# Seven block products in place of eight for the projections vb and g of a hybrid encoder layer

## The chip, the core and the metric

The kernel runs on one core of one Trainium2 chip. The metric is the device time of one execution in microseconds (us). The kernel before has a median of 2027.04 us over three runs, from 2026.38 to 2032.31. One further execution was profiled, and took 2027.01 us.

## What is computed

The input x has 2048 rows (positions) of 1024 channels, in float32. One layer is computed:

```
y = rmsnorm(h, pre_mix_g);  z = y @ w_in
zu, zv, zq, zk, zvb, zg, zlr = split(z)      # widths 512, 512, 256, 256, 512, 512, 16
a = gmlp_mixer(zu, zv, ...)                  # blocks of 128 positions: gelu, layernorm, gate
b = gla_mixer(zq, zk, zvb, zg, zlr, ...)     # a state carried over chunks of 64 positions, times silu(zg)
m = concat(a, b) @ w_out
h = h + rmsnorm(m, post_mix_g)
f = square(relu(rmsnorm(h, pre_ff_g) @ w_ff1)) @ w_ff2
h = h + rmsnorm(f, post_ff_g)
```

The change touches the part `zvb`, `zg` of `z = y @ w_in`: for each block of 512 positions a matrix of 512 x 1024 (y) times one of 1024 x 1024 (the columns of vb and of g).

## The kernel before

The 2048 positions are worked off in four blocks of 512 (loop at L620), each as four tiles of 128. A block runs through stages in this order: vb, q, k, g, then the output projection of the block ahead of it (`out_proj`, L577), then v and u. Block 0 begins with g and vb and has no output projection. After the four blocks come the last output projection and the two feed-forward products, whose seven-product scheme (table `WINO`, L41) was there already.

Each stage is a `product` (L254): eight steps over the inner dimension, and in each step four tiles of three matmuls (`mm3`, L148: a float32 operand is split into a high part of reduced precision and a low rest, and high x low, high x high and low x high are added up). A stage of 512 columns is thus 96 matmuls of 128x512. The weights of a step are read into a staging tile (`stage`, L196: a ring of five, shared with the reads of x), cast by ScalarE to the high part and subtracted by VectorE to the low part (`load_w`, L209), into rings of six tiles each. The weights of q and k are split in block 0 only and written out; later blocks read both parts back (`load_q`, L227).

Results leave PSUM (eight banks, in two rings of four called mm and mx) by `keep` (L601): ScalarE for vb (copy), g (Silu), v and u (Gelu), VectorE for q and k.

Between the steps stand small jobs. `Jobs` (L60) holds generators; `tick` (L91) runs one or two of their steps after each step of a stage, and `finish` (L466) runs them without ticks until a named result is there. `gla` (L324) is the linear attention of one tile, in seven steps. They go from one engine to the next: `gt` on TensorE, then xs, Abs, Exp, Ln, lah and lal (L336 to L345), then `cm` and `dc` on TensorE, then three Exp and qe, ke, then the transposes `qk`, then `sc` and `up`, then `o`, a norm and the transposes `pt`. `spatial` (L435, matmuls `mixd`) and `gate` (L456, transposes `pt` of zu) are the other mixer; `hpost` (L489) closes a tile; `sums` (L534) builds sums of the feed-forward input. `lookup` (L311) puts the loads of ScalarE's function tables where Gelu, Silu and Exp/Ln change.

TensorE's order is the order in which the code is written. The other engines' orders in this part are set by a scheduler when the program is built; each engine and SyncE's queue of transfers then works strictly in that order.

Of the kernel before, what the change touches and what calls it, by code (L numbers as in the profile page):

```python
# [102 lines left out]
def trunk(  # L103
# [24 lines left out]
    q_d = {(g, k): dram.tile([P, 2, n], F32, name=f"{g}_d{k}") for g, n in (("q", 272), ("k", 256)) for k in range(KT)}  # L128

    o_d = [[dram.tile([P, 2, 512], F32, name=f"o_d{hf}_{k}") for k in range(KT)] for hf in range(2)]  # L130
    b_d = [[dram.tile([P, 4, H], F32, name=f"b_d{p}_{k}") for k in range(4)] for p in range(NP)]
    t_d = [{key: dram.tile([P, 2, 2, 512], F32, name=f"t_d{c}_{key}") for key in RIGHT} for c in range(NC)]

# [120 lines left out]
    def product(name, ks, lhs, rhs, evac, steps=1, before=None, tag="mm", later=None):  # L254

        pss = None
        for k in ks:
            if before:
                before(k)
            wh, wl = rhs(k)  # L260
            lh = [lhs(k, t) for t in range(TPB)]
            if pss is None:
                pss = [bank(f"pp_{name}_{t}", tag) for t in range(TPB)]
            for t in range(TPB):
                mm3(pss[t][:, :wh.shape[-1]], *lh[t], wh, wl, k == ks[0], k == ks[-1])
            if k == ks[-1]:
                if later is not None:
                    later.extend((evac, t, pss[t][:, :wh.shape[-1]]) for t in range(TPB))
                else:
                    for t in range(TPB):  # L270
                        evac(t, pss[t][:, :wh.shape[-1]])
            jobs.tick(steps)

    def stats_x(b):

# [190 lines left out]
    def finish(b, part):  # L466

        while b >= 0 and any((i, part) not in ab for i in range(b * TPB, (b + 1) * TPB)):
            if not jobs.step():
                jobs.now += 1  # L470
# [57 lines left out]
    def plus(eng, out_, x_, y_):  # L528
        eng.tensor_tensor(out_, x_, y_, ALU.add)  # L529

    def minus(eng, out_, x_, y_):
        return eng.tensor_tensor(out_, x_, y_, ALU.subtract)
# [82 lines left out]
    def group(b, g, func, before=None, tag="mm", later=None):  # L615
        product(f"{b}_{g}", range(KT), y(b),
                lambda k: load_q(b, g, k) if g in "qk" else load_w(f"{b}_{g}", w_in, GROUPS[g], k),
                keep(b, g, func), 2, before, tag, later)

    for b in range(NB):  # L620
        tiles = range(b * TPB, (b + 1) * TPB)
        if b == 0:
            stats = stats_x(0)


            kept = []
            group(b, "g", AF.Silu, later=kept)

            def before_vb(k):
                if k < 4:  # L630
                    next(stats, None)
                    next(stats, None)
                if k == 4:
                    for _ in stats:
                        pass
                    for evac, t, pst in kept:
                        evac(t, pst)

            group(b, "vb", AF.Copy, before_vb, "mx")
        else:  # L640
            if b == NB - 1:
                jobs.add(*((lambda k=k: sums(0, k), 1) for k in range(4)))
            group(b, "vb", AF.Copy)
        if b == 0:
            with tc.issue_after(loads["0_vb"]):
                consts()
        group(b, "q", None)
        group(b, "k", None)
        if b > 0:
            group(b, "g", AF.Silu, lambda k: finish(b - 1, 1) if k == KT - 1 else None)  # L650
        jobs.add(*((lambda i=i: gla(i), 2) for i in tiles))
        if b > 0:
            out_proj(b - 1)
            jobs.add(*((lambda i=i - TPB: hpost(i), 3) for i in tiles))
# [590 lines left out]
```

## Time and profile before

| what | value |
|---|---|
| median of three runs | 2027.04 us |
| profiled execution | 2027.01 us |
| its span, first to last instruction | 2024.9 us |
| mean granted TensorE clock | 0.995 |
| TensorE busy (matmul) | 1991.8 us, 98% |
| VectorE, ScalarE, GpSimd busy | 1354.9, 928.5, 287.4 us |
| read and written in HBM | 331.45 and 138.54 MB |

PE is TensorE's matmuls, PEld its weight loads, DVE VectorE, ACT ScalarE, POOL GpSimd and SP SyncE, which issues most transfers. A busy time counts every instant at which an instruction of the engine is under way. Since matmuls overlap, the mean duration of one (some 390 ns for 128x512) is longer than the step from one to the next; the steps are read from stretches of time.

### The profile page before, as it was taken

The numbers are of one execution on the slowest core, as the hardware profiler recorded it, in microseconds if no ns is written. First come the engines' busy times: TensorE is split into PE (matmuls) and PEld (weight loads), VectorE is DVE, ScalarE is ACT, GpSimd is POOL, SyncE is SP. The second block draws the span as 40 slices with busy tenths as digits, with TensorE's granted clock in tenths as the row PEclk, the third lists the DMA queues.
The fourth block names the chain that finished last, engine by engine and source line by source line (L and its number), as shares of the span: only waits on it lengthen the run. The fifth ranks groups of instructions, "written<-read, shape, count | busy, mean of one in ns | idle before, by whom it ended". The sixth has DMA issues, their size and how long they took to land.

```text
span 2024.9 us, 27423 instructions
## 1 busy us (share of the span) xinstructions
PE 1991.8 (98%) x9504; PEld 1652.5 (82%) x9504; DVE 1354.9 (67%) x2369; ACT 928.5 (46%) x1846; POOL 287.4 (14%) x464
## 2 busy tenths in 40 slices
PE   8999999999999999999999999999999999999997
PEld 7989888988888887888887888888888887888886
DVE  4483467136724756657678777675888887888887
ACT  5462465136423546556668666665222214222212
POOL 1220312002100200003330333230000003000002
PEclk9999999999999999999999999999999999999999
DMA  7644745635883576758888887787676678867676
GB/s 241 203 131 154 233 157 168 200 135 157 263 281 110 164 278 216 266 171 289 279 280 297 297 291 285 267 278 272 229 257 249 237 275 251 268 246 266 238 266 180
DMA packets 178763, 471.83 MB, mean 233 GB/s; under 512 B 22320, under 2 KB 53568, under 8 KB 164928
## 3 DMA queue, kind: packets, MB, share of 16 engines
q1 hardware_dynamic: 147824, 373.45, 54.4%
q0 software_dynamic: 30800, 96.62, 14.4%
q8 instruction: 75, 1.23, 0.2%
q14 instruction: 64, 0.52, 0.1%
HBM read 331.45 MB, written 138.54 MB: 232 GB/s over the span
## 4 chain that ended last, share of the span: by engine, by line
PE 59%; DVE 1%; DMA 1%; ACT 1%; issue 0%; DVEq 0%; ACTq 0%
PE pf_A L149 6%; PE po_A L149 6%; PE pf_A L151 6%; PE po_A L150 6%; PE po_A L151 6%; PE pf_A L150 6%; PE po_C L149 3%; PE po_C L150 3%; PE po_C L151 3%; PE pf_C L149 3%; PE pf_C L151 3%; PE pf_C L150 3%; PE po_B L149 1%; PE po_B L150 1%; PE po_B L151 1%; PE pf_B L151 1%
## 5 line engine op out<-in xcount | busy, mean ns | idle before, releaser
L529 DVE TENSOR_TENSOR acc<-acc,po_A 128x512 f32<-128x512 f32 x232 | 159.7, 688 | 58.9 <-PE po_A L151 31.9
L980 ACT CAST sh_s<-r 128x512 fp32r<-128x512 f32 x96 | 55.5, 618 | 164.9 <-PE po_A L151 95.1
L980 ACT CAST sh_a<-f 128x512 fp32r<-128x512 f32 x94 | 54.6, 618 | 128.9 <-DMA f<-f_d 87.7
L146 DVE TENSOR_TENSOR wl_s<-s,wh_s 128x512 fp32r<-128x512 f32 x96 | 66.2, 689 | 61.9 <-ACT wh_s L743 61.8
L149 PE MATMUL pf_A<-hl_t,wh_s 128*128 128x512 f32 x256 | 102.0, 398 | 5.1 <-ACT uy L925 2.5
L149 PE MATMUL po_C<-tt,sh_s 128*128 128x512 f32 x256 | 101.2, 395 | 3.3 <-DMA tt<-t_d_t 3.3
L149 PE MATMUL pp_o<-wl_o,abh 128*128 128x512 f32 x256 | 102.9, 402 | 0.9 <-DVE h L486 0.8
L149 PE MATMUL po_A<-tt,sh_s 128*128 128x512 f32 x256 | 100.6, 393 | 1.0 <-DMA tt<-t_d_t 1.0
L151 PE MATMUL pf_A<-hh_t,wl_s 128*128 128x512 f32 x256 | 101.4, 396 | 0.0
L150 PE MATMUL po_C<-tt,sh_s 128*128 128x512 f32 x256 | 100.9, 394 | 0.0
L150 PE MATMUL pf_A<-hh_t,wh_s 128*128 128x512 f32 x256 | 100.7, 393 | 0.0
L151 PE MATMUL po_C<-tt,sl_s 128*128 128x512 f32 x256 | 100.5, 393 | 0.0
L150 PE MATMUL po_A<-tt,sh_s 128*128 128x512 f32 x256 | 100.2, 391 | 0.0
L151 PE MATMUL pp_o<-wh_o,abl 128*128 128x512 f32 x256 | 99.9, 390 | 0.0
L151 PE MATMUL po_A<-tt,sl_s 128*128 128x512 f32 x256 | 99.9, 390 | 0.0
L150 PE MATMUL pp_o<-wh_o,abh 128*128 128x512 f32 x256 | 99.7, 390 | 0.0
L529 DVE TENSOR_TENSOR acc<-acc,po_C 128x512 f32<-128x512 f32 x120 | 82.6, 688 | 23.6 <-PE po_C L151 15.9
L149 PE MATMUL po_A<-tt,sh_a 128*128 128x512 f32 x248 | 97.4, 393 | 0.0
L150 PE MATMUL po_A<-tt,sh_a 128*128 128x512 f32 x248 | 97.1, 391 | 0.0
L151 PE MATMUL po_A<-tt,sl_a 128*128 128x512 f32 x248 | 96.8, 390 | 0.0
L159 POOL TENSOR_TENSOR rs_f<-rs_f,mhalf 128x1 f32<-128x1 f32 x16 | 13.6, 847 | 574.1 <-DVE rs_f L158 574.0
L146 DVE TENSOR_TENSOR wl_a<-w1s,wh_a 128x512 fp32r<-128x512 f32 x96 | 65.9, 687 | 41.7 <-ACT wh_a L743 41.4
(303 smaller groups left out, 5909.2 us busy)
## 6 DMA issues: line engine op xcount, KB each, us to landing
tt<-t_d_t SPq DMA_DIRECT2D x61, 1024.0 KB, 5.2
tt<-t_d_b SPq DMA_DIRECT2D x46, 1024.0 KB, 4.8
w1s<-in_w SPq DMA_DIRECT2D x64, 512.0 KB, 4.9
f<-f_d SPq DMA_DIRECT2D x64, 512.0 KB, 7.1
w2s<-in_w POOLq DMA_DIRECT2D x32, 512.0 KB, 6.3
t_d_t<-th_t POOLq DMA_DIRECT2D x64, 256.0 KB, 5.0
t_d_t<-tl_t POOLq DMA_DIRECT2D x64, 256.0 KB, 4.7
f_d<-ux SPq DMA_DIRECT2D x30, 512.0 KB, 5.5
```

The lines of the kernel that those rows point to most:

```text
L146: v.tensor_tensor(out_lo, src, hi.bitcast(F32), ALU.subtract)
L149: pe.matmul(ps, ahi, blo, start=start, stop=False, **kw)
L150: pe.matmul(ps, ahi, bhi, start=False, stop=False, **kw)
L151: pe.matmul(ps, alo, bhi, start=False, stop=stop, **kw)
L159: pool.tensor_tensor(r, r, mhalf[:, :n], ALU.pow)
L529: eng.tensor_tensor(out_, x_, y_, ALU.add)
L980: a.copy(hi, src)
```

## The change

vb and g of blocks 1 to 3 are computed together, after q and k, as one product of 2x2 blocks with seven products of blocks (`pair`). A block product has four steps of two tiles of three matmuls, 24 in all. Its left operands are blocks of y and four sums of them (s1 to s4), made in q and k from fresh reads of x (`read_s`, `load_s`); its right operands are blocks of the weights and four sums (t1 to t4), which `sums_w` makes once as jobs of block 0 and writes to DRAM. Each of the 28 weight tiles of a pair is read, cast and split. Three PSUM chains, A, B and C, take the products up. Block 0 keeps its eight products. The jobs `sums(0, k)` of block 3 are added after the pair in place of ahead of vb. The new functions and the block loop:

```diff
+    PAIR = ("p1", "p2", "p5", "p6", "p7", "p4", "p3")
+    done_w = []
+    def sums_w(k):
+        bs_ = []
+        for c in range(2):
+            st = wp.tile([P, D], F32, name=f"vs{k}_{c}", tag="xr", bufs=4)
+            dma.dma_start(st, w_in[(k + 4 * c) * P:(k + 4 * c + 1) * P, 1536:2560])
+            bs_.append((st[:, 0:512], st[:, 512:D]))
+        (b11, b12), (b21, b22) = bs_
+        yield 5
+        t1, t2 = (wp.tile([P, 512], F32, name=f"vt{n}_{k}", tag="hts", bufs=2) for n in (1, 2))
+        minus(v, t1, b12, b11)
+        minus(v, t2, b22, t1)
+        minus(v, b12, b22, b12)
+        minus(v, b21, b21, t2)
+        for n, t in enumerate((t1, t2, b12, b21)):
+            dma.dma_start(v_d[k][:, n, :], t)
+        done_w.append(k)
+        yield 1
+    def read_s(b, k):
+        ts = stage(f"xs1_{b}_{k}"), stage(f"xs2_{b}_{k}")
+        for t, kk in zip(ts, (k, k + 4)):
+            dma.dma_start(t, xt[kk * P:(kk + 1) * P, b * TB:(b + 1) * TB])
+        return ts
+    def load_s(b, k, y1, y2):
+        for t, kk in ((y1, k), (y2, k + 4)):
+            a.activation(t, t, AF.Copy, scale=gpre[:, kk:kk + 1])
+        hi = wp.tile([P, D], F32R, name=f"sh{b}_{k}", tag="xr", bufs=4)
+        lo = wp.tile([P, D], F32R, name=f"sl{b}_{k}", tag="h", bufs=4)
+        (a11, a21), (a12, a22) = ((t[:, 0:256], t[:, 256:512]) for t in (y1, y2))
+        plus(v, a22, a21, a22)
+        minus(v, a21, a11, a21)
+        minus(v, a11, a22, a11)
+        minus(v, a12, a12, a11)
+        for n, t in enumerate((y1, y2)):
+            a.copy(hi[:, n * 512:(n + 1) * 512], t)
+            split_lo(lo[:, n * 512:(n + 1) * 512], t, hi[:, n * 512:(n + 1) * 512])
+        return hi, lo
+    def pair(b, ss_):
+        chains = {}
+        zv_, zg_ = {}, {}
+        i0 = b * TPB
+        for m, n in enumerate(PAIR):
+            left, right, chain = WINO[n]
+            begun = chain in chains
+            if not begun:
+                chains[chain] = [bank(f"pv{b}_{chain}{t}", "mx" if chain == "B" else "mm") for t in range(2)]
+            for k in range(4):
+                if right[0] == "t":
+                    st = stage(f"ws_{b}_{n}_{k}")
+                    loads[f"{b}_pair"] = dma.dma_start(st, v_d[k][:, int(right[1]) - 1, :]).ins
+                    wh = wq.tile([P, 512], F32R, name=f"wh_{b}_{n}_{k}", tag="wh", bufs=NW)
+                    wl = wq.tile([P, 512], F32R, name=f"wl_{b}_{n}_{k}", tag="wl", bufs=NW)
+                    a.copy(wh, st)
+                    split_lo(wl, st, wh)
+                else:
+                    wh, wl = load_w(f"{b}_{n}", w_in, GROUPS["vb" if right[2] == "1" else "g"],
+                                    k + 4 * (int(right[1]) - 1))
+                for t in range(2):
+                    if left[0] == "s":
+                        c0 = ("s2", "s3", "s4", "s1").index(left) * 256 + t * P
+                        lh = [z_[:, c0:c0 + P] for z_ in ss_[k]]
+                    else:
+                        c0 = (int(left[1]) - 1) * 256 + t * P
+                        lh = [z_[:, c0:c0 + P] for z_ in ys[b, k + 4 * (int(left[2]) - 1)]]
+                    mm3(chains[chain][t], *lh, wh, wl, k == 0 and not begun, k == 3, skip_group_check=True)
+                if k % 2:
+                    if n == "p6" and k == 3:
+                        finish(b - 1, 1)
+                    jobs.tick(2)
+            r = [rx[b][:, t:t + 1] for t in range(TPB)]
+            A, B, C = (chains.get(c) for c in "ABC")
+            for t in range(2):
+                if n == "p1":
+                    zv_[t] = slot(f"zvb_{i0 + t}")
+                    lookup(zv_[t], A[t], AF.Copy, scale=r[t])
+                elif n == "p2":
+                    v.scalar_tensor_tensor(zv_[t], B[t], r[t], zv_[t], ALU.mult, ALU.add)
+                elif n == "p6":
+                    zg_[t] = slot(f"zg_{i0 + t}", tag="four")
+                    a.copy(zg_[t], A[t])
+                elif n == "p7":
+                    zg_[t + 2] = slot(f"zg_{i0 + t + 2}", tag="four")
+                    a.copy(zg_[t + 2], A[t])
+                    plus(v, zg_[t + 2], zg_[t + 2], C[t])
+                elif n == "p4":
+                    zv_[t + 2] = slot(f"zvb_{i0 + t + 2}")
+                    lookup(zv_[t + 2], A[t], AF.Copy, scale=r[t + 2])
+                elif n == "p3":
+                    plus(v, zg_[t], zg_[t], C[t])
+        for t in range(TPB):
+            lookup(zg_[t], zg_[t], AF.Silu, scale=r[t])
+            z["vb", i0 + t], z["g", i0 + t] = zv_[t], zg_[t]
...
@@ -637,18 +744,32 @@
                         evac(t, pst)
 
             group(b, "vb", AF.Copy, before_vb, "mx")
-        else:
-            if b == NB - 1:
-                jobs.add(*((lambda k=k: sums(0, k), 1) for k in range(4)))
-            group(b, "vb", AF.Copy)
-        if b == 0:
             with tc.issue_after(loads["0_vb"]):
                 consts()
-        group(b, "q", None)
-        group(b, "k", None)
+        ss_, raw = [], []
+        def before_q(k):
+            if b > 0 and k in (2, 5):
+                raw.append(read_s(b, len(raw)))
+        def before_k(k):
+            if b > 0 and k % 2 == 0:
+                ss_.append(load_s(b, k // 2, *raw[k // 2]))
+                if len(raw) < 4:
+                    raw.append(read_s(b, len(raw)))
+        group(b, "q", None, before_q)
+        group(b, "k", None, before_k)
         if b > 0:
-            group(b, "g", AF.Silu, lambda k: finish(b - 1, 1) if k == KT - 1 else None)
+            while len(done_w) < 4:
+                if not jobs.step():
+                    jobs.now += 1
+            pair(b, ss_)
+        if b == NB - 1:
+            jobs.add(*((lambda k=k: sums(0, k), 1) for k in range(4)))
         jobs.add(*((lambda i=i: gla(i), 2) for i in tiles))
+        if b == 0:
+            jobs.add(*((lambda k=k: sums_w(k), 1) for k in range(4)))
         if b > 0:
             out_proj(b - 1)
             jobs.add(*((lambda i=i - TPB: hpost(i), 3) for i in tiles))
```

The end of block 0. TensorE's rows from the last matmul of u on, before: gt is the gate matmul of a gla tile, cm and dc its next step; the numbers behind the names are tile and buffer.

```order
L151 MATMUL pp_0_u_3_1287<-wh_0_u_7_1609,yl_0_7_411 128x512
L334 MATMUL gt2_1633<-gw_218,lrt2_1549 128x256
L334 MATMUL gt3_1647<-gw_218,lrt3_1553 128x256
L149 MATMUL pp_1_vb_0_1672<-wl_1_vb_0_1669,yh_1_0_1323 128x512
L150 MATMUL pp_1_vb_0_1672<-wh_1_vb_0_1668,yh_1_0_1323 128x512
...
L151 MATMUL pp_1_vb_3_1675<-wh_1_vb_2_1722,yl_1_2_1436 128x512
L350 MATMUL cm2_1738<-lal2_1644,trir_224 128x256
```

And now:

```order
L153 MATMUL pp_0_u_3_1295<-wh_0_u_7_1615,yl_0_7_415 128x512
L441 MATMUL gt3_1639<-gw_222,lrt3_1551 128x256
L457 MATMUL cm2_1678<-lal2_1597,trir_228 128x256
...
L463 MATMUL dc2_1683<-trir_228,lah2_1596 128x2
L556 MATMUL mixd2_1702<-zv_2_1251,wt_224 128x128 x4
L457 MATMUL cm3_1717<-lal3_1650,trir_228 128x256
...
L481 MATMUL qk2_1745<-ident_217,qe2_1696 128x128
...
L556 MATMUL mixd3_1754<-zv_3_1253,wt_224 128x128 x4
L151 MATMUL pp_1_q_0_1764<-wl_q1_0_1761,yh_1_0_1332 128x272
```

Between gt3 and cm2, and between cm2 and cm3, stood 36 matmuls of vb and none; now there is nothing between gt3 and cm2, and four small matmuls between cm2's step and cm3's. gt2 has moved one step of u up.

ScalarE at the same place, before (zu is the Gelu of u, e the Abs, Exp and Ln of a gla tile):

```order
L318 ACTIVATE zu_0_1625<-pp_0_u_0_1284,rx0_510 128x512
...
L318 ACTIVATE zu_3_1631<-pp_0_u_3_1287,rx0_510 128x512
L205 ACTIVATE yh_1_7_1662<-xt_1_7_1660,gpre_211 128x512
L338 ACTIVATE e2_1637<-xs2_1635 128x256
L317 ACT_TABLE_LOAD
L318 ACTIVATE e2_1637<-e2_1637 128x256
```

And now:

```order
L310 ACTIVATE xs1_1_1_1963<-xs1_1_1_1963,gpre_215 128x512
L445 ACTIVATE e2_1590<-xs2_1588 128x256
L424 ACT_TABLE_LOAD
L425 ACTIVATE e2_1590<-e2_1590 128x256
L425 ACT_TABLE_LOAD
L425 ACTIVATE zu_0_1631<-pp_0_u_0_1292,rx0_514 128x512
L425 ACT_TABLE_LOAD
L425 ACTIVATE e2_1590<-e2_1590 128x256
L425 ACT_TABLE_LOAD
L425 ACTIVATE zu_1_1633<-pp_0_u_1_1293,rx0_514 128x512
...
L445 ACTIVATE e3_1643<-xs3_1641 128x256
L424 ACT_TABLE_LOAD
```

One table load has become five; Exp and Ln of tile 2 now enclose the first Gelu of u. In the whole program the table loads go from 14 to 18.

VectorE at the end of q in block 2, before: zq takes q out of PSUM, abl is the low part of the transposes pt.

```order
L146 TENSOR_TENSOR abl6_0_3925<-pt6_0_3919,abh6_0_3924 128x512
L146 TENSOR_TENSOR abl7_0_3934<-pt7_0_3928,abh7_0_3933 128x512
L609 TENSOR_SCALAR zq_8_4149<-pp_2_q_0_4021,rx2_3744 128x272
L609 TENSOR_SCALAR zq_9_4151<-pp_2_q_1_4022,rx2_3744 128x272
```

And now (xs1, xs2 are the four blocks of x that become sums, sl their low parts):

```order
L148 TENSOR_TENSOR abl7_0_4111<-pt7_0_4105,abh7_0_4110 128x512
L639 TENSOR_TENSOR xs1_2_2_4202<-xs2_2_2_4203,xs1_2_2_4202 128x256
L639 TENSOR_TENSOR xs2_2_2_4203<-xs2_2_2_4203,xs1_2_2_4202 128x256
L148 TENSOR_TENSOR sl2_2_4293<-xs1_2_2_4202,sh2_2_4292 128x512
L148 TENSOR_TENSOR sl2_2_4293<-xs2_2_2_4203,sh2_2_4292 128x512
L636 TENSOR_TENSOR xs2_2_3_4255<-xs1_2_3_4254,xs2_2_3_4255 128x256
L639 TENSOR_TENSOR xs1_2_3_4254<-xs1_2_3_4254 128x256
L716 TENSOR_SCALAR zq_8_4182<-pp_2_q_0_3982,rx2_3925 128x272
```

The sums of y stand ahead of zq. The transposes pt4 and pt5 stood behind 36 matmuls of vb and now stand behind 36 of q.

## Rows read from the trace of the kernel before

**Rows 1.** Span and granted clock of the core:

```profile
core 0: 2024.9 us, clock 0.995
```

**Rows 2.** What TensorE waited for (total us, times, longest):

```profile
PE pp_g L149 <- ACT yh L205: 6.5, 1, 6.5
PE pp_vb L149 <- ACT zu L318: 0.3, 2, 0.2
```

**Rows 3.** Stretches (us): length, busy by engine (instructions), granted clock, DMA share, GB/s:

```profile
6.50:11.50 5.00, 4.95 (x12) 3.79 (x13) 4.15 (x6) 3.19 (x5) 0.00 (x0) 1.00 0.74 226
136.10:168.70 32.60, 32.60 (x186) 27.20 (x185) 17.05 (x43) 17.35 (x48) 4.21 (x6) 1.00 0.34 94
168.70:194.80 26.10, 25.64 (x212) 25.40 (x211) 10.31 (x25) 6.87 (x18) 2.02 (x2) 1.00 0.56 181
338.30:362.50 24.20, 24.18 (x114) 19.86 (x115) 10.89 (x23) 10.59 (x22) 3.11 (x4) 1.00 0.43 124
362.50:386.00 23.50, 23.50 (x193) 23.50 (x193) 5.52 (x11) 3.80 (x7) 0.00 (x0) 1.00 0.70 216
386.00:407.80 21.80, 21.80 (x98) 18.03 (x97) 3.22 (x6) 5.15 (x7) 0.00 (x0) 1.00 0.63 216
552.60:576.60 24.00, 23.77 (x194) 23.56 (x193) 10.13 (x19) 3.87 (x7) 0.00 (x0) 1.00 0.95 309
```

**Rows 4.** ScalarE in order of time, end of block 0: start, us, instruction:

```profile
134.90 1.84 ACT L318 ACTIVATE zu<-pp_u,rx 128x512 f32<-128x512 f32 x3
138.15 0.71 ACT L205 ACTIVATE yh<-xt,gpre 128x512 fp32r<-128x512 f32 x1
138.77 0.41 ACT L338 ACTIVATE e<-xs 128x256 f32<-128x256 f32 x1
139.19 1.28 ACT L317 ACT_TABLE_LOAD   x1
140.49 0.42 ACT L318 ACTIVATE e<-e 128x256 f32<-128x256 f32 x1
```

**Rows 5.** VectorE at the same place:

```profile
138.04 0.75 DVE L336 TENSOR_TENSOR xs<-gt,gb 128x256 f32<-128x256 f32 x2
141.55 0.43 DVE L341 SCALAR_TENSOR_TENSOR xs<-xs,e 128x256 f32<-128x256 f32 x1 [1.04 <-ACT e L318]
142.01 0.29 DVE L344 CAST lah<-xs 128x256 fp32r<-128x256 f32 x1
142.34 0.43 DVE L146 TENSOR_TENSOR lal<-xs,lah 128x256 fp32r<-128x256 f32 x1
```

**Rows 6.** All engines in order of time, start of vb in block 2:

```profile
337.54 1.84 ACT L318 ACTIVATE zu<-pp_u,rx 128x512 f32<-128x512 f32 x3
338.27 0.50 PE L149 MATMUL pp_vb<-wl_vb,yh 128*128 128x512 f32 x1 [0.17 <-ACT zu L318]
338.27 1.28 DVE L458 TENSOR_TENSOR zu<-zu,zv 128x512 f32<-128x512 f32 x2
339.87 0.69 ACT L318 ACTIVATE zu<-pp_u,rx 128x512 f32<-128x512 f32 x1
344.27 0.49 DVE L462 TENSOR_SCALAR zu<-zu,rs_a 128x512 f32<-128x512 f32 x1 [0.44 <-POOL rs_a L159]
346.92 1.03 PE L303 MATMUL pt<-ident,zu 128*128 128x128 f32 x8
348.04 0.49 DVE L462 TENSOR_SCALAR zu<-zu,rs_a 128x512 f32<-128x512 f32 x1 [0.44 <-POOL rs_a L159]
```

**Rows 7.** VectorE and ScalarE by line, 338.3 to 407.8 us: busy us, mean ns:

```profile
L146 DVE TENSOR_TENSOR wl_g<-ws_g,wh_g 128x512 fp32r<-128x512 f32 x8 | 5.4, 690 | 10.3 <-ACT wh_g L220 10.3
L220 ACT CAST wh_g<-ws_g 128x512 fp32r<-128x512 f32 x8 | 5.0, 621 | 24.0 <-PE pp_k L151 19.8 <-PE pp_g L151 4.2
```

**Rows 8.** Transfers: KB each, median us from issue to landing:

```profile
ws_g<-in_w_in SPq DMA_DIRECT2D x32, 256.0 KB, 3.4
```

**Rows 9.** The page's moved GB/s in 40 slices of 50.6 us:

```profile
GB/s 241 203 131 154 233 157 168 200 135 157 263 281 110 164 278 216 266 171 289 279 280 297 297 291 285 267 278 272 229 257 249 237 275 251 268 246 266 238 266 180
```

## What the change will do

> **What bounds the kernel now.** I read the span and the clock first [rows 1], then what TensorE waits for [rows 2]: over 2024.9 us it has one wait worth naming, 6.5 us at the start, and 0.3 us where u ends and vb begins. So TensorE sets the end, and its order of instructions is fixed: what is taken out of it is gained in full, and every new wait is lost in full, since no slack lies behind it. The stretches [rows 3] give its pace: the g stage of block 2 is 21.8 us for 96 matmuls of 128x512, 0.227 us each; q and k together 23.5 us for 192, q by its columns (272 of 528) some 12.1, 0.126 each. They also show that vb carries other work: in block 2 it is 24.2 us with 16 transposes, and in block 1 the stretch from vb to the end of k (136.1 to 194.8, 58.7 us) holds 110 small matmuls of the jobs beside 288 of the stages. So vb was the cover under which ScalarE and VectorE finished Gelu, gates and attention. That is why I then read the two edges of blocks in order of time [rows 4 to 6].
>
> **The change part by part.**
>
> *Matmuls.* Three pairs of 7 x 24 = 168 replace 192: 72 fewer, 72 x 0.227 = 16.4 us off the path [rows 3].
>
> *From block 0 to block 1.* The jobs of the weight sums take turns from the attention jobs, so that gt3, cm2, dc2, mixd2, cm3, dc3, qk2 and mixd3 now stand together behind the last matmul of u (time T). In the order of ScalarE, tile 2's Exp stands behind the first sums of y and a transfer for the second, landing some 3.4 us after its issue [rows 8]; counting a cast by 0.62 and a scaling by 0.71 [rows 4, 7], Exp ends near T + 2.6. Then come load 1.28, Gelu 0.69, load 1.28 and Ln 0.41 [rows 4, 6], and on VectorE 0.43 + 0.29 + 0.43 [rows 5]: cm2 can start at T + 7.4, and TensorE stands there at T + 0.4. The first wait is 7.0 us; were Exp through at once, 4.0. From that Ln on, ScalarE has load, three Gelu (1.84), Abs, load, Exp, yh and Ln: 1.28 + 1.84 + 0.41 + 1.28 + 0.42 + 0.71 + 0.41 = 6.4; VectorE then xs, qe, lah, ke and lal, 2.0. cm3 is ready 8.4 after the Ln; TensorE came to cm2 1.15 after it and has 12 small matmuls at 0.13, as eight transposes take 1.03 [rows 6]: 1.6. The second wait is 5.6. After it sc2, sc3, pt2 and pt3 have one step of q each as cover (12 x 0.126 = 1.5 us) where vb gave 2.7 to 5.5; counting the queues on I get 1.4, 1.9, 1.5 and 0.4, with nothing as the lower end. That is 17.8 in all. Part of the small matmuls runs while chains are under way, and later waits shrink when earlier ones let VectorE catch up, so I take 14, with 8 and 18 as ends.
>
> What stands behind these waits on ScalarE counts too: the queue holds Gelu of u's other tiles, which free the PSUM banks that q needs. They end before TensorE gets to q, so they cost nothing more.
>
> The load itself [rows 4]: it starts at 139.19, takes 1.28, and the next activation starts at 140.49, so nothing follows it. The Trainium skill, "ScalarE: Activation LUTs", section "What ACT_TABLE_LOAD costs", gives about 2.66 us for a switch, a drain of 1.38 behind the load included. By the rows the five loads here are 6.4 us, by the page 13.3, and the forecast would be 7 us later; the trace does not show the drain.
>
> *q directly behind u, blocks 2 and 3.* q's first step needs the four banks of u, which four Gelu free from 337.54 to 340.56 [rows 6]. vb's matmuls let TensorE pass that in 2.7 us; q's take 1.5, so 1.5 us are lost. Then pt4 to pt7 need the scaled gates: by the rows the second was ready 6.5 us after vb began, the fourth 10.3 (348.04 + 0.49). TensorE is at pt7 after 48 matmuls of q, 12 transposes and the 1.5: 6.0 + 1.6 + 1.5 = 9.1, and waits 1.2. By the new order of VectorE the fourth gate comes a microsecond later; 2.7 to 3.8 are lost by here. Third, zq: between the last gate and zq VectorE has eight operations of 512 columns and seven of 256. The 512 ones start 0.6 apart, as two take 1.28 [rows 6], the 256 ones 0.33, as two take 0.75 [rows 5]: 7.2 us, so zq starts at 17.5 to 18.5, while q ends at 12.1 + 2.1 + 3.3 = 17.5, and k's first matmul waits for zq. That is 0.6 to 2.1. Together 3.3 to 5.9 a block; I take 4.8, two blocks 9.6.
>
> *The pair itself.* A weight tile lasts 6 x 0.227 = 1.36 us in place of 2.73. It costs ScalarE 0.62 and VectorE 0.69 [rows 7], and with the exits each engine is under 28 of some 38 us: covered, if transfers come. A staging tile is bound for 3.4 + 0.62 + 0.69 = 4.7 us, and five give 1.06 tiles per us where 0.73 are used. p6, p7 and p4 follow each other on chain A: p7's first matmul waits until ScalarE has copied the bank (0.69, the Gelu exit of rows 6), while the other half's last three matmuls cover 0.68. Waits of 0.2 stand in rows 2 for such a hand-over, and a cast ahead of the copy would make it 0.9; six joints cost 1.2 to 5.4, I take 2.
>
> *More traffic.* The weight sums read and write 8.4 MB within the first 101 us, where slices of 241 and 203 GB/s [rows 9] make 22.5 MB; together 305 GB/s. In q and k of blocks 2 and 3 eight tiles of x add 2.1 MB to 216 GB/s, again 305. The stretch at 309 GB/s [rows 3] kept TensorE busy for 23.77 of 24.0 us, so both cost little: 0 to 3, I take 1. The sums of block 3 move into the output projection and cost nothing there.
>
> *Restart.* After the 6.5 us of waiting at the start, the first 12 matmuls took 5.0 us [rows 3], 2.3 more than at the later pace, though the granted clock reads 1.00 (2.4 GHz) there. After a 7 us wait this could come again: 0 to 5, I take 1, since waits follow anyway. The Trainium skill, "TensorE: Matmul & The Clock Gate", section "What's actually happening", has TensorE fall to 1.2 GHz when it has been idle; by that the first steps of q in block 1 would be half as fast and the sum 2 to 4 us higher, and the clock row does not show it.
>
> The sum: -16.4 + 14 + 9.6 + 2 + 1 + 1 = +11.2. The profiled execution took 2027.01, as good as the median of 2027.04: 2038 us.
>
> **Rivals.**
>
> *The cover suffices (faster).* The engines that were half idle in vb, q and k (10.9 and 5.5 of some 24 us for VectorE) get ahead, and only joints remain: 2027 - 16.4 + 2 = 2012.6. For it: TensorE waits nowhere today. Against it: the chain at the end of block 0 has serial durations that no idle engine shortens; from 10.3 us of waits on it is not faster by 0.3% any more.
>
> *Floors everywhere.* 8 + 2 x 2.7 + 1.2 = 14.6 against 16.4: 2025. For it: my queues counted by hand may be too strict.
>
> *The pair starves.* If transfers land in 7 us in place of 3.4, five staging tiles give 0.60 per us and a tile lasts 1.66 us: 28 x 0.30 x 3 = 25 more, 2063. For it: 28 tiles a pair where vb and g had 16; against it: 0.26 MB per 1.36 us is 190 GB/s, below the 309 of rows 3.
>
> **How the numbers follow.** The forecast 0.52, its own range 2030 to 2047; floors 0.25; cover suffices 0.13; the pair starves 0.10. A difference of 0.3%, 6.1 us, is about what a measurement of this kernel tells from none. Faster than 2021: the cover rival, 0.13. From 2021 to 2033: the floors and the low edge of the forecast, 0.26. Slower: 0.61. The range for 8 in 10 runs from 2020 to 2050: it leaves out most of the cover rival and the starved pair.
>
> **What would show it.** Right: TensorE's list of waits has cm from VectorE's lal with two entries of 4 to 7 us near 135 to 150, five table loads there, waits of pt for zu and of k for zq near the edges into blocks 2 and 3, and the pair of 168 matmuls at 38 to 39 us. Wrong: no wait over 2 us before 200 us, or pairs above 42 us with waits for staging transfers.

## The result: 33 us slower

The changed kernel takes 2060.06 us (median of five runs, 2058.66 to 2060.59); the kernel before, on the same chip, 2027.22. The ratio is 1.0162, with an interval from 1.0149 to 1.0176. The forecast was 2038, with a range up to 2050: the direction was right, the size a third of what came.

First the span and clock, which answer [rows 1]:

```profile
core 0: 2057.9 us, clock 0.987
```

Then what TensorE waits for, as in [rows 2] (engine, line, what it waited for, and by whom: us in all, times, longest):

```profile
PE cm L457 <- DVE lal L148: 13.6, 2, 9.3
PE pp_q L151 <- ACT zu L425: 7.1, 4, 2.6
PE pp_k L151 <- DVE zq L716: 6.6, 3, 4.1
PE pp_g L151 <- ACT yh L207: 6.0, 1, 6.0
...
PE pp_o L151 <- DVE h L593: 2.3, 1, 2.3
...
PE pp_v L151 <- DVE zk L716: 2.1, 1, 2.1
PE pp_q L151 <- DVE wl_q L148: 1.8, 1, 1.8
```

Of the lines shown, the kernel before had the one at the start (6.5 us) and 0.8 us of pp_o for h. The lines left out are much as they were; the longest (po_C 3.3, pf_A 2.5 and 2.2 us) lie in the feed-forward part and stand in the list of the kernel before too, so "one wait worth naming" was not the whole of that list. The new waits are the predicted kinds (cm for lal, q for Gelu's zu, k for zq), and, in block 0, three that no step of the forecast had: k waiting 4.1 us for zq, v for zk, and q for its weights.

Now the stretches, as in [rows 3]. The first two rows are of the kernel before, of stretches not shown there: q and k of block 0, and from the end of u to the end of k in block 1 (vb, q and k).

```profile
52.70:76.40 23.70, 23.70 (x194) 23.67 (x193) 10.06 (x22) 8.42 (x18) 11.76 (x22) 1.00 0.81 265
135.20:195.00 59.80, 59.34 (x398) 53.26 (x398) 28.46 (x69) 25.16 (x67) 6.23 (x8) 1.00 0.45 137
```

The changed kernel: q and k of block 0; end of u to end of k in block 1; q and k of block 2; its pair; q and k of block 3; the end of the last u to the first feed-forward matmul.

```profile
52.50:84.10 31.60, 25.73 (x193) 25.11 (x191) 12.25 (x26) 7.22 (x17) 14.46 (x28) 0.95 0.98 348
144.20:201.10 56.90, 43.24 (x316) 40.92 (x316) 39.18 (x91) 34.81 (x78) 5.99 (x8) 0.82 0.40 121
359.70:395.10 35.40, 30.55 (x225) 29.93 (x224) 26.12 (x55) 19.67 (x37) 2.71 (x4) 0.90 0.73 215
395.10:434.50 39.40, 39.40 (x170) 31.32 (x169) 20.16 (x31) 21.42 (x34) 0.00 (x0) 1.00 0.63 194
553.50:588.30 34.80, 29.86 (x226) 28.87 (x225) 26.13 (x55) 19.69 (x37) 2.71 (x4) 0.95 0.74 222
744.50:798.50 54.00, 50.83 (x239) 41.73 (x238) 32.99 (x57) 25.56 (x54) 2.18 (x4) 0.97 0.84 293
```

The table shows where the difference lies, stage by stage. Each length runs from the end of one stage's last matmul to the end of the next one's, the last but one to the first feed-forward matmul:

| stage (us) | before | after | difference |
|---|---|---|---|
| q, k of block 0 | 23.7 | 31.7 | +8.0 |
| v, u of block 0 | 58.7 | 60.1 | +1.4 |
| end of u to end of k, block 1 | 59.8 - 21.8 for vb | 56.8 | +18.8 |
| the same, blocks 2 and 3 | 49.7, 50.2 - 21.8 each | 35.5, 34.8 | +7.6, +6.4 |
| vb and g against the pair, three times | 43.6 | 39.3 | -12.9 |
| last u to feed-forward | 48.3 | 54.2 | +5.9 |
| all else | | | -2.2 |

In sum +33.0. Of the -2.2, 1.9 lie in the feed-forward part, which the change leaves alone. The pair itself gains nearly what was forecast; but for the last stretch, to which the section on the prediction comes back, every loss is at a place where the sums are made or where their jobs have pushed other jobs.

How such a loss comes about is seen in block 0, on ScalarE (first line) and VectorE, in order of time (start, duration, and in brackets the idle time before and its releaser):

```profile
56.38 0.42 ACT L222 CAST wh_q<-ws_q 128x272 fp32r<-128x272 f32 x1 [1.14 <-DMA ws_q<-in_w_in]
63.84 0.69 DVE L639 TENSOR_TENSOR vt<-vs 128x512 f32<-128x512 f32 x1 [8.13 <-DMA vs<-in_w_in]
64.45 0.43 DVE L148 TENSOR_TENSOR wl_q<-ws_q,wh_q 128x272 fp32r<-128x272 f32 x1
...
70.25 0.90 DVE L716 TENSOR_SCALAR zq<-pp_q,rx 128x272 f32<-128x272 f32 x2
```

The subtraction of a weight sum stands at the head of VectorE's queue and waits 8.13 us for its 512 KB, while the split of q's last weights (0.43 us) and then the exits of q stand behind it. The cast that this split needs was through at 56.80, so for 7.6 us it waited for its turn alone. The scheduler had put the jobs of v and u there, two stages early. Transfers are slow in that stretch: seen by their issues, the 512 KB reads land after a median of 8.4 us, at 364 GB/s (issue, engine, count, KB each, median us to landing):

```profile
vs<-in_w_in SPq DMA_DIRECT2D x3, 512.0 KB, 8.4
```

### The profile page after: what moved, and what is told of

Its sections match the earlier page's. It is cut to its first block, busy times and chain, and to the rows that moved or that the text cites. A ratio compares the mean times of both kernels' runs of the same rounds, so it can differ in the third digit from the quotient of the medians.

```text
span 2057.9 us, 27751 instructions
## 1 busy us (share of the span) xinstructions
PE 1991.3 (97%) x9432; PEld 1647.9 (80%) x9432; DVE 1434.3 (70%) x2511; ACT 990.9 (48%) x1946; POOL 285.1 (14%) x464
## 4 chain that ended last, share of the span: by engine, by line
PE 58%; DVE 1%; ACT 1%; DMA 1%; issue 0%; DVEq 0%; ACTq 0%
PE po_A L152 6%; PE pf_A L151 6%; PE po_A L151 6%; PE pf_A L153 6%; PE pf_A L152 5%; PE po_A L153 5%; PE po_C L152 3%; PE po_C L151 3%; PE po_C L153 3%; PE pf_C L151 3%; PE pf_C L153 3%; PE pf_C L152 3%; PE po_B L152 1%; PE po_B L151 1%; PE po_B L153 1%; PE pf_B L152 1%
## 5 line engine op out<-in xcount | busy, mean ns | idle before, releaser
L636 DVE TENSOR_TENSOR acc<-acc,po_C 128x512 f32<-128x512 f32 x120 | 82.5, 687 | 23.6 <-PE po_C L153 15.9
L148 DVE TENSOR_TENSOR wl_a<-w1s,wh_a 128x512 fp32r<-128x512 f32 x96 | 65.9, 688 | 40.3 <-ACT wh_a L864 40.1
L148 DVE TENSOR_TENSOR wl_p<-ws_p,wh_p 128x512 fp32r<-128x512 f32 x84 | 57.6, 691 | 51.9 <-ACT wh_p L339 29.8
```

Source lines behind the costliest of these rows:

```text
L148: v.tensor_tensor(out_lo, src, hi.bitcast(F32), ALU.subtract)
```

## The experiments

The theory at the outset: the losses are in-order queues. An instruction of the sums that waits for a transfer, or a job that takes a turn, stands ahead of something that TensorE needs soon. Rivals: the missing cover of vb makes the edges, whatever the sums do; or the work and traffic of the sums has a price wherever they stand. The edge into a block is the stretch from the end of u to the end of k; the same work took 59.8 - 21.8 = 38.0 us in block 1 of the kernel before, and 27.9 in block 2. All ratios are against runs of the kernel before on the same chip in the same session (its medians 2026.84 to 2029.07). The stage lengths of all runs stand together here, in us, for reference. They are of one profiled execution each. For "both spread" and "GpSimd, earlier" it was the slowest one, 6.1 and 3.8 us above the median, and more than half of that lies in the feed-forward part (1264.7 and 1264.0 us against 1261.3 before):

| run | q, k of block 0 | v, u of block 0 | u to k, block 1 | pair, block 1 | u to k, block 2 | pair, block 2 | ratio (interval) |
|---|---|---|---|---|---|---|---|
| before | 23.7 | 58.7 | 59.8 | g 21.8 | 49.7 | g 21.8 | 1 |
| after | 31.7 | 60.1 | 56.8 | 39.3 | 35.5 | 39.3 | 1.0162 (1.0149 to 1.0176) |
| no weight sums | 23.7 | 58.7 | 46.5 | 39.4 | 35.5 | 39.4 | 1.0066 (1.0050 to 1.0082) |
| no sums of y | 30.6 | 60.9 | 52.7 | 38.7 | 27.1 | 38.7 | 1.0075 (1.0051 to 1.0099) |
| neither | 23.7 | 58.7 | 41.0 | 38.7 | 27.1 | 38.7 | 0.9944 (0.9927 to 0.9962) |
| before + weight sums | 29.5 | 63.5 | 77.9 | g 21.8 | 49.9 | g 21.8 | 1.0162 (1.0147 to 1.0177) |
| weight sums held | 23.7 | 60.4 | 59.7 | 44.9 | 35.2 | 39.4 | 1.0174 (1.0154 to 1.0193) |
| sums of y held | 33.0 | 61.7 | 52.8 | 44.8 | 27.1 | 45.7 | 1.0165 (1.0150 to 1.0180) |
| both held | 23.7 | 69.8 | 41.0 | 46.1 | 27.1 | 44.4 | 1.0102 (1.0087 to 1.0117) |
| both spread | 23.7 | 72.8 | 41.1 | 40.0 | 27.2 | 39.7 | 1.0035 (1.0022 to 1.0047) |
| spread, none in q | 23.7 | 73.0 | 41.0 | 46.2 | 27.1 | 44.3 | 1.0105 (1.0088 to 1.0122) |
| GpSimd | 23.7 | 61.1 | 46.6 | 40.3 | 27.3 | 39.8 | 1.0002 (0.9990 to 1.0013) |
| GpSimd, earlier | 23.7 | 66.9 | 40.8 | 40.3 | 27.3 | 39.7 | 1.0017 (1.0008 to 1.0026) |

### Leaving sums out

**No weight sums.**

```diff
-            jobs.add(*((lambda k=k: sums_w(k), 1) for k in range(4)))
-                    ... dma.dma_start(st, v_d[k][:, int(right[1]) - 1, :]).ins
+                    ... dma.dma_start(st, w_in[k * P:(k + 1) * P, <512 columns>]).ins
-            while len(done_w) < 4: ...        # runs jobs ahead of the pair until the sums are there
```

> The changed kernel without the sums of the weights: no reads, subtractions and writes in blocks 0 and 1, and the pair reads plain weights of the same size in place of the sums (left out: the sums of the weights). Theory (queues held up by the weight sums): q and k of block 0 go back by 10 us to about 23.7 us, since nothing stands ahead of their splits in VectorE's queue; the edge from block 0 to block 1 falls from 19 us to about 7, like the edges into blocks 2 and 3, since the attention jobs of tiles 2 and 3 are no longer pushed past the end of u: 2060 - 22 = 2038 us. Rival (the missing cover of vb alone makes the edge): block 0 goes back by 10, the edge stays at 15 to 19: 2046 to 2050.

2041.91 us. Block 0 fell back in full (31.7 to 23.7, and 60.1 to 58.7), and the edge into block 1 by 10.3. The theory's 2038 was 4 too low; 1.5 of that is the edge, which kept a loss of 8.5 us (46.5 - 38.0) and not 7.

**No sums of y.**

```diff
-                ss_.append(load_s(b, k // 2, *raw[k // 2]))
+            pass
-                        lh = [z_[:, c0:c0 + P] for z_ in ss_[k]]
+                        lh = [z_[:, c0:c0 + P] for z_ in ys[b, <plain half>]]
```

> The changed kernel without the sums of y: no reads, scalings, sums, casts and splits of them in q and k, and the pair's products take plain halves of y in their place (left out: the sums of y). Theory (the scaling of the sums, which waits for a transfer, stands ahead of Gelu and of the exits of q in the queues): the edges into blocks 2 and 3 fall from 7.6 and 6.5 us to about 2 each, the edge into block 1 by 3: 2060 - 13 = 2047 us. Rival (what was hidden behind vb has no cover, whatever the sums of y do): the edges stay at 6 to 7 and the time at 2057 to 2060 us.

2044.34 us: the theory. In block 2, q and k go from 35.5 to 27.1 us. (The profiled execution lies at the low end of its four times, which run from 2036.40 to 2046.50, so its stages show more than the median.)

**Neither.** Both edits at once.

> Both left out at once: seven products for vb and g with plain operands, no sums of weights and no sums of y. Theory: the two causes add up, about 2060 - 22 - 13 = 2025 us; what is left is the gain of the pair, 12.9 us, the bare loss of cover behind u, some 7, and 4.7 us in the last output projection. Rival (the loss of cover is the main cost): 2035 us or more. Other rival (they share one wait, so that one alone would already take it away): 2030 us or more, above the sum of both.

2016.0 us, lower than any of the three expected, and 0.9944 of the kernel before. By the medians the two edits save 18.2 and 15.7 us alone and 44.1 together; by the profiled executions 17.8, 23.6 and 44.5, which adds up within 3.2 us. So most of the surplus is the spread of the run without sums of y, whose cause is not known. The two stretches of block 0 and 1 and the two of blocks 2 and 3 (the first row again q and k of block 0, the second the end of u to the end of k in block 1, then q and k of blocks 2 and 3):

```profile
52.10:75.80 23.70, 23.70 (x194) 23.67 (x193) 10.05 (x22) 8.42 (x18) 11.76 (x22) 1.00 0.82 262
...
134.50:175.50 41.00, 39.16 (x301) 37.14 (x302) 25.08 (x63) 19.52 (x57) 6.55 (x8) 0.96 0.48 151
...
333.40:360.40 27.00, 27.00 (x225) 27.00 (x224) 13.36 (x29) 9.02 (x19) 2.48 (x4) 1.00 0.79 245
518.90:545.90 27.00, 27.00 (x225) 27.00 (x225) 13.38 (x29) 9.05 (x20) 2.48 (x4) 1.00 0.81 261
```

TensorE is busy for 27.00 of 27.00 us behind u, without vb. In the kernel before the same work had 49.7 - 21.8 = 27.9 us. So the rival of the missing cover falls for blocks 2 and 3: q alone covers Gelu and the gates. In block 1 it may have 41.0 - 38.0 = 3.0 of the 18.8.

### The weight sums without the pair

**Before + weight sums.** The kernel before, with `sums_w` added as jobs of block 0; its result is not read.

```diff
         jobs.add(*((lambda i=i: gla(i), 2) for i in tiles))
+        if b == 0:
+            jobs.add(*((lambda k=k: sums_w(k), 1) for k in range(4)))
```

> The kernel before, with eight products for vb and g, to which only the sums of the weights are added as jobs of block 0 (their result is written and not read). Theory (VectorE's queue in q and k of block 0 stands behind reads that land late): q and k of block 0 take 31 to 32 us as in the changed kernel, 8 more; the pushed attention jobs find vb's cover in block 1 and cost 0 to 3: 2027 + 8 + 2 = 2037 us. Rival (the pushed jobs cost their 10 us with vb's cover as well): 2045 us.

2059.96 us: both expectations were far too low. These sums alone cost 33 us, as much as the whole change, and the edge into block 1 loses 18.1 with vb's 96 matmuls in place:

```profile
PE cm L372 <- DVE lal L147: 12.6, 2, 8.6
...
PE pp_k L150 <- DVE zq L631: 3.9, 1, 3.9
PE pp_v L150 <- DVE zk L631: 3.9, 1, 3.9
```

The cover is no help, since `cm` of the pushed attention job stands ahead of vb's matmuls in TensorE's own order. So it is the place of the pushed jobs that makes these waits, and not the missing vb, to which the forecast gave a part.

### Holding the sums to a place

**Weight sums held.**

```diff
+            with tc.issue_after(loads["0_v"]):
                 dma.dma_start(st, w_in[...])
-        minus(v, t1, b12, b11)
+        tc.keep_in_program_order(minus(v, t1, b12, b11))
```

> The changed kernel with the weight sums in full, but held to their written place: their reads stay behind the loads of v on SP's queue and their subtractions behind what is written before them on VectorE, so none stands in q and k of block 0. Theory (order of the queue): q and k of block 0 go back by 8 to 10 us, v and u take the traffic at little cost, the edge into block 1 stays near 19 or grows by some us because the sums are later there: 2050 to 2055 us. Rival (the traffic itself costs, wherever it stands): v and u lengthen by what q and k lose, 2058 to 2062 us.

2062.39 us. The first half holds: block 0's q and k go back by 8.0 us exactly, though three of the reads are still issued in k (66.9 to 73.9 us); so it was the place in the queue that cost them. v and u stay as they were (60.4 against 60.1), but they do not take all of the traffic, as the theory had it: only one set of four subtractions runs there, and three run in the edge into block 1, the last up to 193.7 us. No time is won: the edge is 59.7 and the first pair 44.9. TensorE waits 8.9 and 4.3 us for lal again, as the jobs still take their turns, and 3.8 us for the exits of k, which now stand behind sums.

**Sums of y held.**

```diff
-            a.activation(t, t, AF.Copy, scale=gpre[:, kk:kk + 1])
+            r = a.activation(t, t, AF.Copy, scale=gpre[:, kk:kk + 1])
+            tc.keep_in_program_order(r)
-        plus(v, a22, a21, a22)
+        tc.keep_in_program_order(v.tensor_tensor(a22, a21, a22, ALU.add))
```

> The changed kernel with the sums of y in full, but their scalings and first additions held to their written place, behind the Gelu of u on ScalarE and behind the exits of q on VectorE. Theory (place in the queue, not amount of work): q and k of blocks 2 and 3 fall from 35 us to 27.5 to 29, the edge into block 1 by 2 to 4 us, the pair stays under 40 us: 2060 - 15 = 2045 us (2042 to 2048). Rival (the work needs its time wherever it stands, and now the pair's first products that use the sums wait for it): pairs of 42 us or more, 2054 us or more.

2060.07 us: the rival. The edges fall to 27.1 as expected, but the pairs rise to 45.7. The second one's start, VectorE in order of time:

```profile
393.11 0.87 DVE L717 TENSOR_SCALAR zk<-pp_k,rx 128x256 f32<-128x256 f32 x2
...
395.68 0.68 DVE L148 TENSOR_TENSOR wl_p<-ws_p,wh_p 128x512 fp32r<-128x512 f32 x1
...
397.58 1.29 DVE L148 TENSOR_TENSOR sl<-xs,sh 128x512 fp32r<-128x512 f32 x2 [0.28 <-ACT sh L321]
```

k ended at 393.1; on VectorE three sums one after the other have filled k from 382.1 us on, the fourth begins at 393.90 among the exits of k, and the pair's first weight split comes at 395.68.

**Both held.** The same two, and the weight sums called at fixed steps of v and u, without job turns:

```diff
-            jobs.add(*((lambda k=k: sums_w(k), 1) for k in range(4)))
+                if act == 0:
+                    ws_[k] = sums_w(k)
+                next(ws_[k])        # from the steps of v and u of block 0
```

> The full computation of the changed kernel, with both sets of sums held to place: the sums of y as in the run above, and the sums of the weights called at fixed steps of v and u of block 0, behind v's loads, without taking turns from the attention jobs. Theory: q and k of block 0 24 us, edge into block 1 until the end of k 41 to 44 us in place of 57, q and k of blocks 2 and 3 28 us, pairs 39.5: 2060 - 8 - 14 - 14 = 2024 us (2019 to 2030), the bare pair's 2016 and some us more. Rival (block 0 has no room for the sums: v and u lengthen by the 8 us that q and k lose, or the edge stays at 50 us or more): 2032 to 2040 us.

2047.69 us. The edge into block 1 is 41.0, as in the run with neither: the 15.8 us there were turns and queues, since both sums are made in full here. But v and u grew by 11 and the pairs by 5 to 7. On SyncE's queue, near the end of u (start, and time to issue):

```profile
128.80 0.33 SPq L298 DMA_DIRECT2D v_d<-vt  x1
129.46 0.33 SPq L215 DMA_DIRECT2D ws_u<-in_w_in  x1
```

The load of u's weights stands behind a write that waits for VectorE's vt, and on VectorE their split, at 135.39, behind four more subtractions; TensorE waited 4.9 us for it.

**Both spread.** Weight sums in eight free buffers and in place, their writes issued some steps after; sums of y at step 7 of q, steps 0 and 3 of k, and one behind the pair's first two weight tiles.

```diff
+                    if (7, 8, 11, 18)[k] == n:      # steps of q, k and pair
+                        ss_.append(load_s(b, k, *raw[k]))
+                    if (1, 4, 6, 9)[k] == n:
+                        raw.append(read_s(b, k))
```

> The full computation of the changed kernel with both sets of sums spread out. Weights: eight buffers that are free in block 0, sums made in place, reads at steps 2, 4, 6 and 8 of v and u, subtractions three steps later, writes four to two steps after those, so that no load on SP's queue stands behind a buffer or a subtraction. Sums of y: read at steps 1, 4, 6 of q and 1 of k, made at step 7 of q, steps 0 and 3 of k and behind the first two weight tiles of the pair. Theory (each loss of the run with both sums held to place, 11 us in v and u of block 0 and 6 at each pair, is an in-order queue behind a wait, not work that does not fit): v and u of block 0 59 to 61 us, q and k of blocks 2 and 3 27 to 29, pairs 39 to 41: 2018 to 2024 us. Rival (the sums are too much work for these stretches): v and u stay at 65 us or more, pairs at 44: 2040 us or more.

2035.52 us. The sums of y are nearly free now: 27.2 and 39.7, against 27.1 and 38.7 without them. v and u did not follow (72.8). **Spread, none in q**, the same with steps (8, 10, 13, 18) and reads at (2, 5, 7, 10):

> As the run with both sums spread out, but the sums of y are made at steps 0, 2 and 5 of k and behind the first two weight tiles of the pair, none in q, with reads at steps 2, 5, 7 of q and 2 of k. Theory: q and k of blocks 2 and 3 at 27.1 us, pairs 1 to 3 us longer than with one sum in q, since VectorE is free between the last gate and the exits of q and that gap is lost here: 2020 to 2027 us. Rival (what counts is only that nothing stands ahead of the exits of q): as fast as or faster than that run.

2049.95 us, pairs of 46.2 and 44.3: with this sum moved from q into k they are 6.2 and 4.6 us longer, more than the 1 to 3 us expected.

**GpSimd.** As both spread, with the subtractions and writes of the weight sums on GpSimd and its queue, and reads two steps later.

```diff
-        tc.keep_in_program_order(minus(v, b11, b12, b11))
+        tc.keep_in_program_order(minus(pool, b11, b12, b11))
...
+            tc.keep_in_program_order(pool.dma_start(v_d[k][:, n, :], t))
```

> As the run with both sums spread out, with two edits to the weight sums: the 16 subtractions and the 16 writes move from VectorE and SP's queue to GpSimd and its queue, and the reads start two steps later (steps 4, 6, 9, 11 of v and u of block 0). Theory (v and u of block 0 lose 14 us there because reads issued in a burst land late ahead of v's weights, and because VectorE, busy for 13 to 14.5 of 15 us in u, puts the sums ahead of u's splits): v and u fall from 72.8 us to 59 to 62 and the time to 2024 us (2019 to 2029), about that of the kernel before or a little below. Rival (it is the traffic of 8.4 MB, whoever makes the sums): v and u stay at 68 us or more, 2034 us or more. Other rival (GpSimd is slower and holds back the square roots of the norms): the wait only changes its name, v and u at 64 to 70 us.

2029.24 us: the first version level with the kernel before, v and u 61.1 us. So block 0 has room for the traffic. The edit moved three things at once (the engine, the queue of the writes, the reads by two steps); that VectorE's queue was the main one is seen in u of the run before, "both spread", where the split of a weight tile comes 11.8 us after its cast is through and TensorE waits 6.3 us for it:

```profile
122.79 0.62 ACT L222 CAST wh_u<-ws_u 128x512 fp32r<-128x512 f32 x1 [1.81 <-DMA ws_u<-in_w_in]
135.20 0.68 DVE L148 TENSOR_TENSOR wl_u<-ws_u,wh_u 128x512 fp32r<-128x512 f32 x1
135.94 0.80 PE L151 MATMUL pp_u<-wl_u,yh 128*128 128x512 f32 x1 [6.27 <-DVE wl_u L148]
```

A subtraction takes 1.46 to 1.48 us on GpSimd against 0.69 on VectorE. The edge into block 1 was 46.6, as the last sums ran into it: u ended at 137.6, and the square root rs_a of a gate, for which `cm` then waits 3.3 us, stands behind the last writes. While the subtractions run, some of VectorE's own operations take longer too: three gate products 4.80 us here, where two take 1.28 [rows 6].

```profile
137.74 4.80 DVE L573 TENSOR_TENSOR zu<-zu,zv 128x512 f32<-128x512 f32 x3
143.63 2.16 POOL L300 DMA_DIRECT2D v_d<-vs  x4
145.80 0.57 POOL L161 TENSOR_TENSOR rs_a<-rs_a,mhalf 128x1 f32<-128x1 f32 x1
```

**GpSimd, earlier**, by one to two steps:

> As the run with the weight sums on GpSimd, but one to two steps earlier in v and u of block 0 (reads at steps 3, 5, 7, 9, the last write at step 13 in place of 15), since there the last sums ran from 137 to 146 us, behind the end of u, ahead of the square roots of the gates in GpSimd's queue. Theory: the stretch from the end of u to the end of k in block 1 falls from 46.6 to 41 or 42 us, v and u stay at 59 to 62, and the time is 2023 us (2019 to 2027), below the kernel before. Rival (the sums only push other square roots now, those of the norms in u): v and u at 64 us or more, 2027 to 2032 us.

2030.83 us. The edge fell to 40.8, as the theory said, and v and u rose to 66.9, as the rival said. Whether it is for the rival's reason, the square roots, is not shown: TensorE's waits in v and u are 3.2 us for the split of u's weights and 2.3 for the exits of k. No version that makes all the sums was faster than the kernel before.

### Block 3's sums

The run with neither, and `sums(0, k)` ahead of q again.

```diff
+            if b == NB - 1:
+                jobs.add(*((lambda k=k: sums(0, k), 1) for k in range(4)))
         ss_, raw = [], []
```

> The pair with plain operands, without sums of weights and sums of y (left out: both), and with the sums for block 3's right-hand side queued ahead of q again, as in the kernel before, in place of behind the pair. Theory (these sums, moved to the last output projection, delay the exits of its banks): the stretch from the end of u to the feed-forward part falls from 51.3 us back to 48.3, the time from 2016 to 2013 us. Rival (what stretches it is something else): 51 us and 2016.

2023.16 us, ratio 0.9982 (0.9973 to 0.9992). The last stretch stayed at 51.8 (51.3 without the edit), and q and k of block 3 rose from 27.1 to 34.7. Neither number was expected. The move out of q saves 7.6 us there, and undoing it does not shorten the last output projection.

## Why the prediction was wrong

**Matmuls and joints: right.** -16.4 + 2 forecast, -12.9 measured. The transfers of the pair never starved, so that rival falls too.

Term by term, measured less forecast: matmuls and joints +1.5, traffic +8.4, the edge into block 1 +4.8, q behind u +4.4, restart -1 (it lies in the others), the last stretch +5.9, all else -2.2; that is the 21.8 us between +11.2 and +33.0.

**"More traffic": the step that failed.** It weighed the weight sums by GB/s alone ("both cost little: 0 to 3, I take 1"). They cost 8.0 us in q and k of block 0 and 1.4 in v and u, and both go when the sums are left out. The order of VectorE's instructions is fixed when the program is built; it has a subtraction that waits for 512 KB ahead of a split of q's weights. What was missing was to ask what stands behind an instruction that waits, and to take a landing time from a stretch near the top of the GB/s row: 8.4 us, where [rows 8] had 3.4.

**From block 0 to block 1: right in kind, short by 4.8.** Forecast 14, measured 18.8, with cm waiting 9.3 and 4.3 us for lal where 7.0 and 5.6 were worked out by hand. The first is longer since tile 2's Exp ended at 149.14, 4.9 us behind the last matmul of u and not 2.6: the casts of the first sum of y, ahead of it on ScalarE, had waited 1.46 us for VectorE. From there to cm it was 5.0 us, 4.8 by hand. The later waits (sc, pt) that made 5.2 us of the sum were nothing. In their place came TensorE's clock: between the two waits and behind the second, the granted clock is 0.50, that is 1.2 GHz:

```profile
154.20:162.20 8.00, 3.74 (x16) 3.45 (x16) 4.81 (x10) 7.44 (x17) 0.87 (x1) 0.50 0.09 23
162.30:166.50 4.20, 4.20 (x21) 4.20 (x21) 3.48 (x10) 3.29 (x10) 1.52 (x2) 0.50 0.05 19
```

By an estimate half of these 7.94 busy us, some 4, is lost: eight of the `mixd` matmuls take 2.05 us here, and sixteen took 1.95 at 1.00 in the kernel before. The cause was only half named as well: the forecast blamed the turns of the jobs and the missing cover; the runs show that the turns do it with or without the cover.

**q directly behind u: a fair size, two of its three terms by the wrong mechanism.** 9.6 forecast, 14.0 measured. The third term, k waiting for zq behind the sums on VectorE, came as forecast (0.9 and 1.6 us where 0.6 to 2.1 were taken). The first two, banks and gates, were put down to the missing cover; TensorE did wait for the banks, 3.9 and 3.2 us, but not for that reason, and for the gates hardly. Gates and Gelu have no loss of their own there (27.0 us, all busy). It is the sums of y in the queues. On ScalarE at the edge into block 2:

```profile
359.45 0.72 ACT L310 ACTIVATE xs<-xs,gpre 128x512 f32<-128x512 f32 x1 [2.44 <-DMA xs<-in_xt]
362.11 1.14 ACT L320 CAST sh<-xs 128x512 fp32r<-128x512 f32 x2 [1.94 <-DVE xs L639]
363.16 0.68 ACT L425 ACTIVATE zu<-pp_u,rx 128x512 f32<-128x512 f32 x1
364.65 0.72 ACT L310 ACTIVATE xs<-xs,gpre 128x512 f32<-128x512 f32 x1 [0.81 <-DMA xs<-in_xt]
365.28 1.82 ACT L425 ACTIVATE zu<-pp_u,rx 128x512 f32<-128x512 f32 x3
```

The first Gelu stands behind a scaling and two casts of a sum that the pair first uses in its third product, some 40 us later; q waits for the bank. Without these sums the edge is free, so at these two edges "the cover suffices" was wrong because of what the change itself queued ahead.

**Restart: 1 forecast, some 12 measured.** The same matmuls of blocks 2 and 3 keep TensorE busy for 30.55 and 29.86 us in place of 27.00 without the sums of y, those of block 0's q and k for 25.73 in place of 23.70, at granted clocks of 0.90, 0.95 and 0.95; with the 4 us above, 3.6 + 2.9 + 2.0 + 4 = 12.5, all behind waits. They are part of the losses in the table, not on top. Not every wait is followed by the lower clock: after the 2.1 us that v waited for zk the row reads 1.00. The 1.00 of [rows 3] at the start, on which the forecast leaned, does not show full speed either. There the matmuls of 128x512 stand 0.43 us apart, nearly twice the pace of 0.227, just as behind the wait of pp_o for h, where the clock of the stretch is 0.60 (first line: kernel before; the others: changed kernel):

```profile
7.14 0.63 PE L150 MATMUL pp_g<-wh_g,yh 128*128 128x512 f32 x1
774.63 0.63 PE L151 MATMUL pp_o<-wl_o,abh 128*128 128x512 f32 x1
773.80:778.00 4.20, 4.17 (x11) 3.30 (x12) 4.11 (x7) 3.20 (x9) 0.00 (x0) 0.60 1.03 385
86.20:90.00 3.80, 3.76 (x17) 3.03 (x18) 2.92 (x7) 0.74 (x2) 0.00 (x0) 1.00 0.93 326
```

The Trainium skill, "TensorE: Matmul & The Clock Gate", section "What's actually happening", says that an idle TensorE falls to 1.2 GHz; the forecast put this rule aside by one stretch with a clock of 1.00, and by that rule its sum would have been 2 to 4 us higher at this one edge. The trace agrees: 0.50 there.

**The table load: as the rows had it.** There are five loads at the edge into block 1, as forecast; each takes 1.28 us, stands 0.02 us or less behind the activation ahead of it, and is followed by the next one after 0.02. One of them:

```profile
150.44 0.69 ACT L425 ACTIVATE zu<-pp_u,rx 128x512 f32<-128x512 f32 x1
151.15 1.28 ACT L425 ACT_TABLE_LOAD   x1
152.44 0.42 ACT L425 ACTIVATE e<-e 128x256 f32<-128x256 f32 x1
```

The Trainium skill, "ScalarE: Activation LUTs", section "What ACT_TABLE_LOAD costs", adds a drain of 1.38 us to each; this trace has none, ahead of a load or behind it.

**Sums of block 3: 0 forecast, the stretch +5.9.** The run that put the sums back ahead of q shows that this does not shorten it. The traces have three parts that make it up. Sixteen more `mixd` matmuls run in this stretch, 1.8 us, which ran ahead of the end of u before (kernel before, then changed kernel):

```profile
L449 PE MATMUL mixd<-zv,wt 128*128 128x128 f32 x16 | 1.9, 275 | 0.0
L556 PE MATMUL mixd<-zv,wt 128*128 128x128 f32 x32 | 3.7, 275 | 0.0
```

The waits for VectorE's h are 2.3 + 0.9 us in place of 0.8, which is 2.4; and 4.2 us at a clock of 0.60 behind the longer one cost some 1.7 by an estimate. With the sums back ahead of q these `mixd` go back as well, but there the stretch, at 51.8, still has a wait of 1.8 us for h. Why h comes late stays open.

## What to carry to other kernels

Added side work is not priced by its busy time or its bytes but by what stands behind it in each in-order queue: look in the new order for every added instruction that waits for a transfer, and count the wait against the next thing that the critical engine needs. Here the scheduler put consumers of transfers two stages and more ahead of where they were written; give such work a place by hand, reads well ahead, one piece at a time into gaps. And a wait of the matmul engine can be paid twice, the second time in clock: some 12 of the 33 us here.

## What the runs showed that was not expected

Side work alone, with no change on the critical engine, can cost as much as the whole change: 33 us for 16 subtractions (16 x 0.69 = 11 us of VectorE) and 8.4 MB. The scheme itself is worth 0.9944 with plain operands, and with all the sums it is at 1.0174 to 1.0002 in eight orders of the same sums: their place decides over 35 us, but no order tried keeps any of the gain. And reads of 512 KB took 8.4 us to land at 364 GB/s, where the 256 KB of [rows 8] took 3.4.
